# A gated-attention driver: fixed waits of TensorE's tasks replaced by the driver's own estimate

## The chip, the cores and the metric

The kernel runs on one core of a Trainium2 chip. The metric is the device time of one execution in microseconds (us), as the median of several runs. A core has five engines that matter here. TensorE (PE in the rows, its weight loads PEld) multiplies matrices out of SBUF into the banks of PSUM. VectorE (DVE) does elementwise work and scans, ScalarE (ACT) does activations and copies, GpSimd (POOL) helps with elementwise work, and SyncE (SP) issues most DMAs. Each engine runs its own list of instructions in program order and waits on semaphores for the others.

## What is computed

One inference step of a two-layer network for 128 context rows and 512 latent rows, 640 together. Each layer has a normalisation with modulation, one input projection, a neighbourhood attention, a gated linear attention (GLA) with two directions, an output projection and an MLP. The change touches only TensorE's order in the GLA. Its reference, cut to what matters:

```python
def gla_chunked(q, k, v, logf, s0):                      # chunks of 64 rows
    def step(S, inp):
        qi, ki, vi, fi = inp
        b = jnp.cumsum(fi, axis=-2)
        diff = b[..., :, None, :] - b[..., None, :, :]
        decay = jnp.exp(jnp.where(causal, diff, -jnp.inf))
        attn = jnp.einsum('bhid,bhjd,bhijd->bhij', qi, ki, decay)
        o = jnp.einsum('bhij,bhje->bhie', attn, vi) + jnp.einsum('bhid,bhde->bhie', qi * jnp.exp(b), S)
        b_last = b[..., -1:, :]
        S = jnp.exp(b_last)[..., 0, :, None] * S + jnp.einsum('bhjd,bhje->bhde', ki * jnp.exp(b_last - b), vi)
        return S, o
...
def gla_bidir(q, k, v, lf, lb, sf0, sb0):
    of, sf = gla_chunked(q, k, v, lf, sf0)
    ob, sb = gla_chunked(flip(q), flip(k), flip(v), flip(lb), sb0)
    return (of + flip(ob)).astype(v.dtype), sf, sb
```

The kernel works with chunks of 128 rows and gets the decayed products of a chunk by halving: level 64 multiplies the two halves of a chunk with each other, level 32 the halves of the halves, and so on through 16, 8, 4, 2, 1 and 0.

## The kernel before

**Projections.** A projection unit multiplies the 1024 rows of the weights of 128 output columns with the activations. It has eight steps, and each step is six matmuls, three weight loads by two parts of the 640 columns (`mm3`, L614). In the profile they write `ps_mm` from `row` and `wh` or `wl`, the high and low half of the split weights. ScalarE makes `wh` and, in the attention, VectorE makes `wl` (`prepare`, L483).

**The driver.** TensorE's order is not left to a scheduler: it is the order in which Python issues its instructions. `Drv` (L51) keeps an estimated TensorE time `dv.t`. `filler` (L119) runs a projection unit step by step, and after each step it lets waiting tasks issue their matmuls, for at most 1.8 us of estimated time. A task is a generator. Where it yields a number it comes back that many us later by `dv.t`; where it yields a name and a count it waits until so many units of that resource are free. `dv.rel(name, n, lat)` gives units back `lat` us later. The resource "sm" stands for the four small PSUM banks `ps_sm`. Which real bank a tile gets is a fixed rotation through the four.

**The estimate.** `Est` (L130) notes every instruction as it is issued and puts it into a list of slots for its engine, from a fixed cost and a cost by element; a slot may go into a hole between earlier ones. `until(tiles)` (L179) says how long from `dv.t` until the tiles are written, plus 0.6 us; `free(tiles)` (L183) says how long until their last reader is done. The tasks of the neighbourhood attention already use both; the tasks of the GLA use fixed numbers. The orders of VectorE and ScalarE come from a scheduler that sorts by priority and readiness, so they follow when TensorE's order moves.

**The GLA task.** `gla_pair` (L1129) runs for two heads at a time, twice in each layer (pair 0 and pair 1). Its steps, with the names that stand in the rows:

- gates: matmuls `ps_sm<-row,wg`, then on ScalarE and VectorE logarithms and scans into `PN`, and the scaled keys `ks`
- states, once for each direction: transposes `ps_sm<-ident,ks`, a copy to `ksT`, products `ps_sm<-gv,ksT`, and four updates of `ST` on VectorE (in layer 1 the tile lies in `cbc`, and the rows say `cbc`)
- levels 64 to 0: for each, `level_vec` (L1112) makes `ex` with two subtractions `ex<-PN`, an exponential on ScalarE and a product `ex<-ex,qk`; then TensorE multiplies `ps_sm<-ex`. Levels 64, 32 and 16 share four banks, the others take two each. `A` and `Dg` collect the results, on VectorE from level 4 on. Level 0 uses `q,qk`
- output: `ps_sm<-qs,ST` and `ps_sm<-A,gv`, then per head a sum of squares `ps_mm<-sqo,ones`

Around it run transposes of values (`ps_sm<-ident,gt` into `gv` or `V`), in layer 0 the modulation of later stages on VectorE (`ada_step`, L569, a pair of instructions `junk<-wr,cbc` and `wr<-wr,cbc`), and the rotary step of each query or key unit (`gla_rope`, L1060: a shuffle, two products and a sum on `tmp`, 512 wide).

Of the kernel before, what the change touches and what calls it, by code (L numbers as in the profile page):

```python
# [212 lines left out]
class Kern:  # L213
# [915 lines left out]
    def gla_pair(self, l, pr):  # L1129
        nc, gp, dv = self.nc, self.gp, self.dv  # L1130
# [5 lines left out]
        for d in range(2):  # L1136
            yield ("sm", 2)
            ps = [self.smp.tile([128, 512], F32, name="ps_sm", tag="sm")[:, 0:hi - lo] for lo, hi in self.HALF]
            for (lo, hi), t in zip(self.HALF, ps):
                nc.tensor.matmul(t, lhsT=self.wg[0:64, l, d, 128 * pr:128 * pr + 128],  # L1140
                                 rhs=self.zT[0:64, lo:hi], start=True, stop=True)
            dv.pe(1.07)
            bc = (PC_BGF if d == 0 else PC_BGB) + 2 * l + pr
            bcol = self.pc[:, bc:bc + 1]
            mn = gp.tile([128, T], F32, name="tmp", bufs=5)
            sp = gp.tile([128, T], F32, name="tmp", bufs=5)
            for (lo, hi), t in zip(self.HALF, ps):
                nc.scalar.activation(out=sp[:, lo:hi], in_=t, func=AF.Abs, bias=bcol)
                nc.vector.tensor_scalar(out=mn[:, lo:hi], in0=t, scalar1=bcol, scalar2=0.0, op0=ALU.add, op1=ALU.min)
            dv.rel("sm", 2, 1.4)  # L1150
            nc.scalar.activation(out=sp, in_=sp, func=AF.Exp, scale=-1.0)
            nc.scalar.activation(out=sp, in_=sp, func=AF.Ln, bias=1.0)
            if d == 0:
                for c in range(5):
                    s = slice(128 * c, 128 * c + 128)
                    nc.vector.tensor_tensor_scan(out=PN[:, 0, s], data0=mn[:, s], data1=sp[:, s], initial=0.0,
                                                 op0=ALU.add, op1=ALU.subtract)
                nc.vector.tensor_copy(tot[:, 0], PN[:, 0].rearrange("p (c t) -> p c t", c=5)[:, :, 127])
            else:
                nc.vector.memset(PN[:, 1].rearrange("p (c t) -> p c t", c=5)[:, :, 0:1], 0.0)  # L1160
                for c in range(5):
                    s = slice(128 * c, 128 * c + 127)
                    nc.vector.tensor_tensor_scan(out=PN[:, 1, 128 * c + 1:128 * c + 128], data0=sp[:, s],
                                                 data1=mn[:, s], initial=0.0, op0=ALU.add, op1=ALU.subtract)
                last = lambda t: t.rearrange("p (c t) -> p c t", c=5)[:, :, 127]
                nc.vector.tensor_tensor(out=tot[:, 1], in0=last(mn), in1=last(sp), op=ALU.subtract)
                nc.vector.tensor_tensor(out=tot[:, 1], in0=tot[:, 1], in1=last(PN[:, 1]), op=ALU.subtract)
# [5 lines left out]
        ks = gp.tile([128, 2, T], F32, name="ks", tag="ex", bufs=3)  # L1173
        cv = lambda t: t.rearrange("p (c t) -> p c t", c=5)
        nc.vector.tensor_tensor(out=cv(ks[:, 0]), in0=tot[:, 0, :, None].to_broadcast([128, 5, 128]), in1=cv(PN[:, 0]),
                                op=ALU.subtract)
# [3 lines left out]
        if l == 0:  # L1180
            ST = gp.tile([128, 2, 5, 128], F32, name="ST")
        else:

            ST = self.cbc.rearrange("p r k -> p (r k)")[:, 0:1280].rearrange("p (d c e) -> p d c e", d=2, c=5)
        nc.scalar.dma_start(out=ST[:, 0, 0], in_=self.a["state_fwd"][l, pr])
        nc.scalar.dma_start(out=ST[:, 1, 3], in_=self.a["state_bwd"][l, pr])
        vecs = {64: self.level_vec(64, PN, qk), 32: self.level_vec(32, PN, qk)}
        yield 13.0
        while not all(("gv", 2 * pr + i) in self.done for i in range(2)):
            yield 1.0  # L1190

        for d in range(2):
            chunks = (0, 1, 2, 4) if d == 0 else (3, 2, 1, 4)
            yield ("sm", 1)
            pt = self.smp.tile([128, 512], F32, name="ps_sm", tag="sm")
            for i, c in enumerate(chunks):
                nc.tensor.transpose(pt[:, 128 * i:128 * i + 128], ks[:, d, 128 * c:128 * c + 128], self.ident)
            dv.pe(0.43)
            kt = gp.tile([128, 512], F32, name="ksT", bufs=1)
            nc.scalar.activation(out=kt, in_=pt, func=AF.Copy)  # L1200
            dv.rel("sm", 1, 0.9)
            if d == 1:
                vecs[16] = self.level_vec(16, PN, qk)
            yield 1.0
            yield ("sm", 1)
            up = self.smp.tile([128, 512], F32, name="ps_sm", tag="sm")
            for i, c in enumerate(chunks):
                for hh in range(2):
                    hv = 128 * (2 * pr + hh)
                    nc.tensor.matmul(up[64 * hh:64 * hh + 64, 128 * i:128 * i + 128],  # L1210
                                     lhsT=kt[:, 128 * i + 64 * hh:128 * i + 64 * hh + 64],
                                     rhs=self.gv[:, c, hv:hv + 128], start=True, stop=True)
            dv.pe(0.95)
            for i, c in enumerate(chunks):
                u = up[:, 128 * i:128 * i + 128]
                if c == 4:
                    nc.vector.tensor_copy(ST[:, d, 4], u)
                    nc.scalar.dma_start(out=self.o["new_sf" if d == 0 else "new_sb"][l, pr], in_=ST[:, d, 4])
                else:
                    nxt = c + 1 if d == 0 else c - 1  # L1220
                    nc.vector.scalar_tensor_tensor(out=ST[:, d, nxt], in0=ST[:, d, c], scalar=dtot[:, d, c:c + 1],
                                                   in1=u, op0=ALU.mult, op1=ALU.add)
            dv.rel("sm", 1, 1.3)


        A = gp.tile([128, 10, 128], F32, name="A")
        Dg = gp.tile([128, 10, 32], F32, name="Dg")
        lv = (64, 32, 16, 8, 4, 2, 1, 0)
        qs = None
        for n, s in enumerate(lv):  # L1230

            if s == 64:
                yield ("sm", 4)
                aps = [[self.smp.tile([128, 512], F32, name="ps_sm", tag="sm") for _ in range(2)] for _ in range(2)]
            if s < 16:
                yield ("sm", 2)
                dps = [self.smp.tile([128, 512], F32, name="ps_sm", tag="sm") for _ in range(2)]
            kt, qt = vecs.pop(s)
# [36 lines left out]
                    mi = {4: 1, 2: 2, 1: 3, 0: 4}[s]  # L1275
                    nc.vector.copy_predicated(Dh, self.masks[:, mi, None, :].to_broadcast([128, 5, 32]), v5(dps[hh]))
            if s == 16:
                dv.rel("sm", 4, 1.5)
            elif s < 16:
                dv.rel("sm", 2, 0.9)  # L1280

            if n + 3 < len(lv) - 1:
                vecs[lv[n + 3]] = self.level_vec(lv[n + 3], PN, qk)
# [4 lines left out]
            elif n + 3 == len(lv):  # L1288

                qs = gp.tile([128, 2, NS], F32, name="qs", tag="ex", bufs=3)  # L1290
# [3 lines left out]
                                        in1=cv4(PN[:, 1, :NS]), op=ALU.add)  # L1294
                nc.scalar.activation(out=qs[:, 1], in_=qs[:, 1], func=AF.Exp, scale=1.0 / 16)
                nc.vector.tensor_tensor(out=qs, in0=qs, in1=qk[:, 1:2, :NS].to_broadcast([128, 2, NS]), op=ALU.mult)
            if s > 0:
                yield 2.0
        for g in range(4):
            gs = slice(32 * g, 32 * g + 32)  # L1300
            nc.vector.copy_predicated(A[gs, :, gs], self.masks[gs, 0, None, :].to_broadcast([32, 10, 32]), Dg[gs])
        self.done.add(("qk", pr))
        yield 3.0


        yield ("sm", 3)
        op = [self.smp.tile([128, 512], F32, name="ps_sm", tag="sm") for _ in range(2)]
        opp = self.smp.tile([128, 512], F32, name="ps_sm", tag="sm")
# [16 lines left out]
        for hh in range(2):  # L1325
# [1 line left out]
            nc.scalar.activation(out=og[:, :NS], in_=op[hh], func=AF.Copy)  # L1327
            nc.scalar.activation(out=og[:, NS:T], in_=opp[:, 128 * hh:128 * hh + 128], func=AF.Copy)
            ogs.append(og)
        dv.rel("sm", 3, 1.8)  # L1330
        self.done.add(("gla", pr))

        for hh in range(2):
            h = 2 * pr + hh
            og = ogs[hh]
            sq = gp.tile([128, T], F32, name="sqo", tag="tmp", bufs=5)
            nc.scalar.activation(out=sq, in_=og, func=AF.Square)
            yield 3.0
            yield ("mmx", 1)
            ps = self.mmp.tile([128, 1024], F32, name="ps_mm", tag="mm")  # L1340
            for lo, hi in ((0, 256), (256, T)):
                nc.tensor.matmul(ps[:, 256 + lo:256 + hi], lhsT=self.ones, rhs=sq[:, lo:hi], start=True, stop=True)
            dv.pe(1.07)
            rs = gp.tile([128, T], F32, name="tmp", bufs=5)
            nc.scalar.activation(out=rs, in_=ps[:, 256:896], func=AF.Ln, scale=1.0 / 128, bias=self.eps)
            dv.rel("mmx", 1, 1.2)
            nc.scalar.activation(out=rs, in_=rs, func=AF.Exp, scale=-0.5)
            nc.vector.tensor_tensor(out=og, in0=og, in1=rs, op=ALU.mult)
            while ("gate", h) not in self.done:
                yield 1.0  # L1350
            nc.vector.tensor_tensor(out=self.gg[h], in0=self.gg[h], in1=og, op=ALU.mult)
# [540 lines left out]
```

## Time and profile before

| | us |
|---|---|
| three runs | 1685.94, 1687.76, 1692.98 |
| median | 1687.76 |
| the profiled execution, as timed | 1693.68 |
| its span, first to last instruction | 1692.0 |
| TensorE busy in the span | 1621.8 |
| VectorE busy | 1228.6 |
| ScalarE busy | 749.7 |
| GpSimd busy | 424.2 |

The mean granted TensorE clock is 0.981 of full speed. TensorE's idle time is read as the length of a stretch minus its busy time. A stretch with a granted clock of 0.50 runs at 1.2 GHz instead of 2.4 GHz, so half of its busy time is lost. GLA pair 0 of layer 0 lies at about 71 to 150 us of the span, pair 1 at 151 to 235; in layer 1 they lie at 918 to 1003 and 1009 to 1083.

### The profile page before, as it was taken

The numbers are of one execution on the slowest core, as the hardware profiler recorded it, in microseconds if no ns is written. First come the engines' busy times: TensorE is split into PE (matmuls) and PEld (weight loads), VectorE is DVE, ScalarE is ACT, GpSimd is POOL, SyncE is SP. The second block draws the span as 40 slices with busy tenths as digits, with TensorE's granted clock in tenths as the row PEclk, the third lists the DMA queues.
The fourth block names the chain that finished last, engine by engine and source line by source line (L and its number), as shares of the span: only waits on it lengthen the run. The fifth ranks groups of instructions, "written<-read, shape, count | busy, mean of one in ns | idle before, by whom it ended". The sixth has DMA issues, their size and how long they took to land.

```text
span 1692.0 us, 32606 instructions
## 1 busy us (share of the span) xinstructions
PE 1621.8 (96%) x13544; PEld 1549.0 (92%) x13544; DVE 1228.6 (73%) x2300; ACT 749.7 (44%) x1224; POOL 424.2 (25%) x178
## 2 busy tenths in 40 slices
PE   8989798999999999999998899999989999999999
PEld 6988697879999999999997798988889999999998
DVE  5686968888797779777677858487796675666653
ACT  4545345644443223322345455466366444443441
POOL 1100000013344444444345000000123344343342
PEclk9998899999999999999999999999999999999999
DMA  9122243342454444444242111222221222132222
GB/s 375 52 66 79 83 144 103 98 132 97 157 178 132 154 154 148 140 149 163 78 146 67 55 54 58 95 68 76 78 71 63 74 77 88 63 100 75 76 89 87
DMA packets 61347, 179.28 MB, mean 106 GB/s; under 512 B 6928, under 2 KB 17808, under 8 KB 61200
## 3 DMA queue, kind: packets, MB, share of 16 engines
q1 hardware_dynamic: 45360, 159.76, 28.2%
q10 hardware_dynamic: 15840, 17.45, 3.4%
q8 instruction: 107, 1.75, 0.4%
q14 instruction: 40, 0.33, 0.1%
HBM read 170.36 MB, written 6.82 MB: 105 GB/s over the span
## 4 chain that ended last, share of the span: by engine, by line
PE 73%; DVE 17%; ACT 5%; issue 3%; DMA 2%; POOL 1%; ACTq 0%; DVEq 0%; POOLq 0%
PE ps_sm L198 37%; PE ps_mm L198 35%; DVE ex L198 2%; DVE s L198 2%; DVE row L198 2%; DVE sqa L198 1%; DVE wl L198 1%; ACT wh L198 1%; DVE junk L198 1%; PE ps_ss L198 1%; DVE y L198 1%; DVE wr L198 1%; ACT s L198 1%; DVE tmp L198 1%; DVE m L198 1%
## 5 line engine op out<-in xcount | busy, mean ns | idle before, releaser
L198 POOL TENSOR_TENSOR wl<-wr,wh 128x1024 fp32r<-128x1024 f32 (+1 forms) x148 | 396.3, 2683 | 1195.8 <-ACT wh L198 1184.2
L198 PE MATMUL ps_mm<-row,wh 128*128 128x256 f32 (+2 forms) x2192 | 444.8, 323 | 6.6 <-DVE row L198 3.6
L198 ACT ACTIVATE wh<-wr 128x1024 fp32r<-128x1024 f32 (+1 forms) x209 | 214.9, 1028 | 485.8 <-PE ps_sm L198 272.3
L198 PEld LDWEIGHTS ps_mm<-row,wh 128*128 128x128 f32 x2192 | 361.3, 194 | 27.4 <-issue 17.2
L198 PE MATMUL ps_mm<-row,wl 128*128 128x256 f32 (+2 forms) x1096 | 258.2, 314 | 0.5 <-DVE wl L198 0.5
L198 PEld LDWEIGHTS ps_mm<-row,wl 128*128 128x128 f32 x1096 | 202.8, 193 | 0.7 <-DVE wl L198 0.7
L198 PE MATMUL ps_sm<-row,wh 128*128 128x322 f32 (+2 forms) x736 | 153.9, 312 | 0.0
L198 ACT ACTIVATE r<-r 128x512 f32<-128x512 f32 (+2 forms) x192 | 113.7, 618 | 59.8 <-DVE r L198 57.0
L198 DVE SCALAR_TENSOR_TENSOR ar<-ar,cbc 128x1024 f32<-128x1024 f32 x56 | 124.9, 2238 | 1.0
L198 PEld LDWEIGHTS ps_sm<-row,wh 128*128 128x128 f32 x736 | 122.3, 190 | 0.0
L198 PE MATMUL ps_sm<-uh,wh 128*128 128x256 f32 (+1 forms) x512 | 119.0, 308 | 0.0
L198 PE MATMUL ps_mm<-uh,wh 128*128 128x256 f32 (+1 forms) x512 | 118.9, 308 | 0.0
L198 PE MATMUL ps_mm<-ul,wh 128*128 128x256 f32 (+1 forms) x512 | 118.6, 308 | 0.0
L198 PE MATMUL ps_sm<-ul,wh 128*128 128x256 f32 (+1 forms) x512 | 118.5, 307 | 0.0
L198 PE MATMUL ps_mm<-uh,wl 128*128 128x256 f32 (+1 forms) x512 | 118.5, 307 | 0.0
L198 PE MATMUL ps_sm<-uh,wl 128*128 128x256 f32 (+1 forms) x512 | 118.5, 307 | 0.0
L198 DVE SCALAR_TENSOR_TENSOR row<-ps_sm,mod,row 128x256 f32<-128x256 f32 (+1 forms) x216 | 81.6, 430 | 50.2 <-PE ps_sm L198 50.2
L198 DVE TENSOR_TENSOR r<-ps_sm,r 128x322 f32<-128x322 f32 x98 | 46.9, 490 | 93.6 <-PE ps_sm L198 55.4
L198 DVE SCALAR_TENSOR_TENSOR row<-ps_mm,mod,row 128x128 f32<-128x128 f32 (+2 forms) x180 | 89.1, 533 | 31.0 <-PE ps_mm L198 31.0
L198 PE MATMUL ps_sm<-m,wh 128*128 128x322 f32 x480 | 99.2, 312 | 0.0
L198 PE MATMUL ps_sm<-row,wl 128*128 128x322 f32 (+2 forms) x368 | 99.0, 311 | 0.0
L198 DVE TENSOR_TENSOR wl<-wr,wh 128x1024 fp32r<-128x1024 f32 (+2 forms) x69 | 73.2, 1061 | 30.5 <-ACT wh L198 29.6
(222 smaller groups left out, 3067.4 us busy)
## 6 DMA issues: line engine op xcount, KB each, us to landing
wr<-w_dn SPq DMA_DIRECT2D x68, 512.0 KB, 3.5
wr<-w_up SPq DMA_DIRECT2D x64, 512.0 KB, 3.5
ar<-w_ada SPq DMA_DIRECT2D x56, 512.0 KB, 3.7
wr<-w_in SPq DMA_DIRECT2D x48, 512.0 KB, 3.6
wr<-w_ada SPq DMA_DIRECT2D x24, 512.0 KB, 3.5
wa<-w_ada SPq DMA_DIRECT2D x16, 512.0 KB, 10.2
wr<-w_o SPq DMA_DIRECT2D x16, 512.0 KB, 3.5
tab<-bias ACTq DMA_DIRECT2D x32, 96.0 KB, 2.9
```

Source lines behind the costliest of these rows:

```text
L198: r = f(*args, **kw)
```

## The change

All waits of `gla_pair` that were numbers become calls of the estimate. The two waits that stood at the end of a level (2.0 us, and none ahead of level 64) become one ahead of each level, for that level's own `ex` tiles. `dv.pe` and all arithmetic stay as they are.

```diff
-            dv.rel("sm", 2, 1.4)
+            dv.rel("sm", 2, self.est.free(*ps))
...
-        yield 13.0
+        yield self.est.until(ks)
...
-            dv.rel("sm", 1, 0.9)
+            dv.rel("sm", 1, self.est.free(pt))
             if d == 1:
                 vecs[16] = self.level_vec(16, PN, qk)
-            yield 1.0
+            yield self.est.until(kt)
...
-            dv.rel("sm", 1, 1.3)
+            dv.rel("sm", 1, self.est.free(up))
...
         for n, s in enumerate(lv):
+            yield self.est.until(*vecs[s])
...
             if s == 16:
-                dv.rel("sm", 4, 1.5)
+                dv.rel("sm", 4, self.est.free(*aps[0], *aps[1]))
             elif s < 16:
-                dv.rel("sm", 2, 0.9)
+                dv.rel("sm", 2, self.est.free(*dps))
...
-            if s > 0:
-                yield 2.0
...
-        yield 3.0
+        yield self.est.until(A, qs, ST)
...
-        dv.rel("sm", 3, 1.8)
+        dv.rel("sm", 3, self.est.free(*op, opp))
...
-            yield 3.0
+            yield self.est.until(sq)
...
-            dv.rel("mmx", 1, 1.2)
+            dv.rel("mmx", 1, self.est.free(ps))
```

**First place: TensorE, layer 0, pair 0, where the scaled keys are transposed.** Before, the transposes of the value tile `gt` stand alone, and those of `ks` come seven projection steps later:

```order
L198 MATMUL ps_mm<-row_7_278,wh 128x384
L198 MATMUL ps_mm<-row_6_277,wl 128x256
L198 MATMUL ps_mm<-row_6_277,wl 128x384
L198 MATMUL ps_sm<-ident,gt 128x128 x5
L198 MATMUL ps_mm<-row_0_279,wh 128x256
```

Now the same place reads:

```order
 L198 MATMUL ps_mm<-row_6_277,wl 128x256
 L198 MATMUL ps_mm<-row_6_277,wl 128x384
+L198 MATMUL ps_sm<-ident,gt 128x128 x4
+L198 MATMUL ps_sm<-ident,ks 128x128 x4
+L198 MATMUL ps_sm<-ident,gt 128x128
+L198 MATMUL ps_mm<-row_0_279,wh 128x256
```

The transposes of `ks` moved seven steps of six matmuls forward, in between those of `gt`.

**Second place: VectorE, layer 0, pair 0, between the state updates and level 8.** Before, the last two updates of `ST` stand behind steps of the rotary work of the next key unit (`tmp`):

```order
L198 SCALAR_TENSOR_TENSOR ST<-ST,dtot,ps_sm 128x128 x2
L198 STREAM_SHUFFLE tmp<-tmp 128x512
L198 SCALAR_TENSOR_TENSOR ST<-ST,dtot,ps_sm 128x128
L198 TENSOR_TENSOR tmp<-tmp,sin 128x512
L198 TENSOR_TENSOR tmp<-tmp,cos 128x512
L198 TENSOR_TENSOR ex<-ex,qk 128x1280
L198 TENSOR_TENSOR qk<-tmp 128x512
L198 COPY ST<-ps_sm 128x128
```

Now all of `ST` stands ahead of this, and the rotary work falls between the vectors of levels 8 and 4 (the first `ex<-ex,qk` is level 8's product, the second level 4's):

```order
L198 SCALAR_TENSOR_TENSOR wr,mod_110<-wr,cbc 128x1024
L198 TENSOR_TENSOR ex<-PN 128x640 x2
L198 TENSOR_TENSOR wl<-wr,wh 128x1024
L198 TENSOR_TENSOR ex<-PN 128x640
L198 TENSOR_TENSOR ex<-ex,qk 128x1280
L198 TENSOR_TENSOR ex<-PN 128x640
L198 STREAM_SHUFFLE tmp<-tmp 128x512
L198 COPY A<-ps_sm 128x512
L198 TENSOR_TENSOR tmp<-tmp,sin 128x512
L198 TENSOR_TENSOR tmp<-tmp,cos 128x512
L198 TENSOR_TENSOR ex<-ex,qk 128x1280
```

The state moved out from behind the rotary work, and level 4's product moved behind it.

**Third place: TensorE, layer 1, pair 0, level 8 at the same projection step.** Before, level 8 stands here alone, with transposes of `gt` on both sides, and level 4 comes three steps later:

```order
L198 MATMUL ps_mm<-row_2_9007,wl 128x384
L198 MATMUL ps_sm<-ident,gt 128x128 x4
L198 MATMUL ps_sm<-ex 32x32 x40
L198 MATMUL ps_sm<-ident,gt 128x128 x5
L198 MATMUL ps_mm<-row_4_9009,wh 128x256
```

Now (40 of the 80 are level 8, 40 are level 4):

```order
L198 MATMUL ps_mm<-row_2_9007,wl 128x256
L198 MATMUL ps_mm<-row_2_9007,wl 128x384
L198 MATMUL ps_sm<-ex 32x32 x80
L198 MATMUL ps_mm<-row_4_9009,wh 128x256
L198 MATMUL ps_mm<-row_4_9009,wh 128x384
```

Level 4 moved up behind level 8, with no projection step between them, and the transposes of `gt` moved away.

## Rows read from the trace of the kernel before

**Rows 1.** The page's first line: the span of the profiled execution.
```profile
span 1692.0 us, 32606 instructions
```

**Rows 2.** Windows, by stage: length, then busy (count) of PE, PEld, DVE, ACT, POOL; PEclk.
```profile
82.60:138.90 56.30, 48.12 (x877) 44.53 (x875) 50.66 (x81) 24.16 (x33) 0.00 (x0) 0.94 0.26 82
152.20:220.70 68.50, 57.99 (x923) 52.84 (x922) 62.02 (x104) 33.55 (x50) 0.00 (x0) 0.90 0.26 84
941.40:986.00 44.60, 41.93 (x836) 38.49 (x834) 34.37 (x58) 16.70 (x24) 0.00 (x0) 0.96 0.17 53
1009.00:1070.00 61.00, 57.71 (x945) 53.46 (x946) 49.77 (x82) 32.34 (x50) 0.00 (x0) 0.97 0.19 59
250.00:400.00 150.00, 138.14 (x1062) 120.99 (x1060) 128.13 (x348) 77.67 (x167) 11.73 (x5) 0.97 0.35 110
1105.00:1205.00 100.00, 96.16 (x795) 82.63 (x794) 81.19 (x248) 62.96 (x143) 2.37 (x1) 1.00 0.27 83
```

**Rows 3.** TensorE's waits, 82 to 225 us: us in total, times, longest us.
```profile
PE ps_sm L198 <- DVE ST L198: 12.6, 3, 5.8
PE ps_sm L198 <- DVE V L198: 2.5, 1, 2.5
PE ps_sm L198 <- DVE A L198: 1.7, 1, 1.7
PE ps_sm L198 <- DVE Dg L198: 1.3, 2, 1.1
```

**Rows 4.** TensorE's waits, 941.4 to 1075 us.
```profile
PE ps_sm L198 <- DVE cbc L198: 2.5, 2, 1.3
PE ps_sm L198 <- DVE A L198: 2.0, 1, 2.0
```

**Rows 5.** Windows of the stretches in which TensorE's clock was lowered.
```profile
101.90:108.60 6.70, 5.61 (x36) 5.19 (x44) 4.00 (x6) 1.27 (x1) 0.00 (x0) 0.50 0.03 10
139.50:149.60 10.10, 10.10 (x51) 8.98 (x51) 0.82 (x1) 2.15 (x5) 0.00 (x0) 0.50 0.11 36
180.40:190.60 10.20, 4.49 (x21) 4.40 (x22) 8.05 (x13) 3.34 (x5) 0.00 (x0) 0.50 0.36 118
207.70:211.00 3.30, 3.30 (x89) 2.90 (x89) 3.23 (x7) 1.58 (x2) 0.00 (x0) 0.50 0.02 5
1047.40:1050.70 3.30, 3.30 (x83) 2.89 (x83) 3.26 (x6) 1.27 (x1) 0.00 (x0) 0.50 0.34 134
```

**Rows 6.** Timeline of TensorE: level 64's second part, a gate stage, one level.
```profile
102.99 0.48 PE L198 MATMUL ps_sm<-ex 64*64 64x64 f32 x6 [4.56 <-DVE ST L198]
...
1008.88 2.42 PE L198 MATMUL ps_sm<-row,wg 64*128 64x256 f32 x8
...
1027.16 0.60 PE L198 MATMUL ps_sm<-ident,ks 128*128 128x128 f32 x4
...
1041.02 0.89 PE L198 MATMUL ps_sm<-ex 64*32 64x32 f32 x80
```

**Rows 7.** Window of 18 projection steps (108 matmuls), of tile ps_mm alone.
```profile
1011.20:1027.40 16.20, 16.10 (x108) 15.84 (x108) 0.00 (x0) 2.73 (x4) 1.00 0.09 35
```

**Rows 8.** Groups of VectorE's instructions, 82 to 140 us: busy, mean ns.
```profile
L198 DVE TENSOR_TENSOR ex<-PN 128x640 f32<-128x640 f32 x13 | 10.5, 849 | 2.2 <-PE ps_sm L198 2.2
...
L198 DVE SCALAR_TENSOR_TENSOR junk<-wr,cbc 128x1024 bf16<-128x1024 f32 x4 | 4.9, 1216 | 0.0
...
L198 DVE SCALAR_TENSOR_TENSOR ST<-ST,dtot,ps_sm 128x128 f32<-128x128 f32 x6 | 2.0, 340 | 0.0
```

**Rows 9.** Timeline of VectorE in layer 1, pair 1.
```profile
1022.41 1.48 DVE L198 TENSOR_TENSOR ks<-ks,qk 128x1280 f32<-128x1280 f32 x1
1023.81 1.48 DVE L198 TENSOR_TENSOR ex<-ex,qk 128x1280 f32<-128x1280 f32 x1
1025.21 1.21 DVE L198 TENSOR_TENSOR wl<-wr,wh 128x1024 fp32r<-128x1024 f32 x1
1026.35 1.48 DVE L198 TENSOR_TENSOR ex<-ex,qk 128x1280 f32<-128x1280 f32 x1
```

## The prediction

> **What bounds the kernel now.** I began with the page and went to the stages that the change touches. The profiled execution has a span of 1692.0 us [rows 1] and was timed at 1693.68; the median of the three runs shown is 1687.76, some 6 us less. I make the sum in us gained or lost against this one execution and take it off the median as it stands.
>
> The windows by stage [rows 2] show what can be won. TensorE's idle time is the length less its busy time. In GLA pair 0 of layer 0 (82.6 to 138.9) that is 56.30 - 48.12 = 8.18 us, in pair 1 68.50 - 57.99 = 10.51, in layer 1 2.67 and 3.29: 24.65 us together. The same rows show who is late: VectorE is busy 50.66 of 56.30 us and 62.02 of 68.50 in layer 0. In layer 1, which has no modulation work there, it is 34.37 of 44.60 and 49.77 of 61.00. So in layer 0 TensorE waits beside a VectorE that is nearly full; TensorE's order can move such waits, but it can only remove those in which VectorE did something that nobody was waiting for.
>
> The lists of TensorE's waits say the same by name. In layer 0, 12.6 us are for `ST` [rows 3], in three pieces of which one is 4.56 at 102.99 [rows 6]. That is level 64 waiting for the bank whose last reader is the state update. `V` (2.5), `A` (1.7) and `Dg` (1.3) follow [rows 3]. In layer 1 the waits are `cbc`, the state again, with 2.5, and `A` with 2.0 [rows 4].
>
> The third thing to read is the clock. Five stretches by these waits ran at a granted 0.50, the lower level of 1.2 GHz [rows 5]. Half of their busy time is lost: 5.61 / 2 = 2.8 and 10.10 / 2 = 5.05 by pair 0, 2.25 and 1.65 by pair 1, 1.65 in layer 1. The 10.10 is the whole output stage of pair 0, which follows the wait for `A` of 1.7. The losses now are thus 8.18 + 2.8 + 5.05 = 16.0, 10.51 + 3.9 = 14.4, 2.67, and 3.29 + 1.65 = 4.94: 38.0 us. Nothing before 82 us moves, and behind the GLA the order is the same again, so all of the change's effect lies in these 38 us and in what takes their place.
>
> **The prices.** A projection step costs 16.10 / 18 = 0.9 us [rows 7], a level of 32-row products 0.9, a set of key transposes 0.6, a gate stage 2.4 [rows 6]; I take a state product as a level, 0.9. On VectorE a subtraction for a level costs 10.5 / 13 = 0.8, a modulation instruction 1.2, a state update 0.3, and so does a `Dg` copy by its nearness [rows 8]. A level's product costs 1.4 from start to start (1022.41 to 1023.81), a `wl` 1.14 [rows 9]. A 512-wide step is an estimate from the 640-wide one, four fifths of 0.8, or 0.65. With these I walk down the changed order of TensorE and VectorE side by side. Where VectorE's sum is longer than TensorE's between the same two points, the difference is a wait.
>
> **Layer 0, pair 0.** The keys are transposed seven steps earlier, level 64 stands three steps earlier (53 instead of 56, in steps from the start of the projections) and the output seven (73 instead of 80). All state updates now stand ahead of the rotary work, so the 4.56 us and the low clock behind it go; about 0.4 remain, inside the rounding. New waits come at the levels. From level 64 to level 4 VectorE has two modulation instructions, four subtractions, one `wl`, two products and four 512-wide steps, now that the rotary work stands ahead of level 4's product: 2.4 + 3.2 + 1.14 + 2.8 + 2.6 = 12.1 us. TensorE has four levels, level 64 taken as one of them, and five steps: 3.6 + 4.5 = 8.1. It waits 4.0, shared by levels 8 and 4. To level 2: 0.65 + 3.2 + 1.4 = 5.25 against 0.9 + 2.7 = 3.6, a wait of 1.65. To level 0, which now stands right behind level 1 and needs the banks that level 2's `Dg` copies free: 1.4 + 0.9 + 0.5 + 2.4 + 1.14 + 2.3 = 8.6 against 0.9 + 4.5 + 0.9 = 6.3, a wait of 2.3. To the output both have 8.0. That is 8.0 us of waits. Each is as long as those that were followed by a lowered clock, but while TensorE is waiting for VectorE anyway a slow TensorE only shortens the next wait; I count one low stretch, the last, with 1.65. The output's 5.05 I take as gone, since hardly any wait is left ahead of `A`; its other bound is that all of it stays. Pair 0 loses 9.7 instead of 16.0: **a gain of 6.3**.
>
> **Layer 0, pair 1.** Here the keys come 11 steps behind the gates instead of 14. From the gate matmuls (1008.88) [rows 6] to the end of the keys' product (1022.41 + 1.48) [rows 9] layer 1 needed 15.0 us with much the same VectorE list. TensorE has 2.4 + 11 x 0.9 = 12.3: a wait of 2.7, where there was none, and 1.65 of clock. Up to the last state update VectorE has five subtractions, two `wl`, three products, two modulation pairs, a gate product and eight small ones: 4.0 + 2.3 + 4.2 + 4.8 + 0.8 + 2.4 = 18.5, against 12.0 of TensorE (nine steps, transposes, state products, the first part of level 64) and 1.65 for the low clock. So level 64 still waits, 4.8, and 1.65 of clock follow. Level 2 then gets the two banks of a value transpose. VectorE copies the second of them to `V` only after eight subtractions and four products, 19.5 in all, against 15.3: 4.2 and 1.65. Together 16.65 instead of 14.4: **a loss of 2.25**.
>
> **Layer 1.** In pair 0 levels 8 and 4 now follow each other with no step between. VectorE needs 3.2 + 2.8 + 0.65 + 1.14 = 7.8 for both, and some 0.8 for ScalarE's exponential, against 6.3: a wait of 2.3, 1.65 of clock, 0.4 at level 2, or 4.35 instead of 2.67. In pair 1 the keys come 11 steps behind the gates instead of 18; the 15.0 us were measured here, and VectorE's list between is unchanged, so the wait is 2.7, with 1.65 of clock. The second value transposes wait 2.45 for the banks of the first. That is 6.8 instead of 4.94. **Losses of 1.7 and 1.9.**
>
> The rest of the diff has one answer: the wait ahead of the sums of squares and the bank returns move matmuls that stand in projection work with nobody behind them, and SyncE's and GpSimd's lists are unchanged.
>
> **Sum.** 6.3 - 2.25 - 1.7 - 1.9 = 0.45 us gained: 1692.0 becomes 1691.6 of span, and 1687.76 becomes 1687.3. The measurement tells apart about 0.5%, or 8.4 us, so this is no change.
>
> **The rivals.**
>
> *The estimate holds (faster).* The neighbourhood attention already takes its waits from this estimate. In layer 1 it idles 3.84 of 100 us, in layer 0 11.86 of 150 beside a VectorE that is busy 128.13 [rows 2]. If the GLA's 230.4 us came to the first share, idle time would fall from 24.65 to 8.8, and clock losses of 13.4 in proportion by 8.6: 24.4 us, or 1663.4. At the second share it is 6.4 + 3.5 = 9.9, or 1677.9. Against it: the neighbourhood tasks have several independent units to choose from, a GLA pair is one chain. Chance 0.20.
>
> *Each new wait costs the clock as well (slower).* I count twelve new waits, and six low stretches as hidden. If these are not hidden, 6 x 1.65 = 9.9 us come on top, and if the output of pair 0 stays at 1.2 GHz, 5.05: 15 us, or 1702. The output and three of the six are enough to make it measurably slower (8.4 + 0.45 = 8.9). For it speaks that waits of 1.7 and 2.0 have such a stretch behind them [rows 3 to 5]; against it, that the slowed work lies ahead of a further wait for VectorE. The Trainium skill (Perfetto Trace Analysis, Matmul Optimizations) says that the engine scales with its use and that matmuls should stand back to back in batches; the rows agree, and by it alone this rival would be the likelier. Chance 0.18.
>
> *The banks decide (nothing happens).* Of the 18.7 us in layer 0's waits, 12.6 + 2.5 + 1.3 = 16.4 end with the reader of a small bank, not with a missing operand [rows 3]. Four banks in fixed rotation may keep every wait at its size wherever it stands: 1687.8. The Trainium skill (Perfetto Trace Analysis, Optimization Strategy) reads gaps that repeat as a sign that PSUM or SBUF is short for the next tile; by this rule the order brings nothing. Against it: the 4.56 us came from VectorE's order. Chance 0.17.
>
> **How the numbers follow.** The forecast has 0.45. With the banks' rival it makes 0.62 for no measurable change, 0.20 for faster, 0.18 for slower. The range takes the lower half of the gain at the second share, some 4 us below 1677.9 for my rounding, down to 1674, and the slower rival's beginning, up to 1697.
>
> **What would show it.** Right: level 64 of layer 0's pair 0 waits under 1 us for `ST`; the output stage there runs at full clock; both second pairs show a wait of 2 to 3 us at `ps_sm<-ident,ks`; layer 1 has a wait of about 2 us at level 4 of pair 0. Wrong: no wait at the keys (then the estimate holds), idle time in the four stretches far from 24.65, or the output stage of layer 0's pair 0 still at a granted 0.50.

## The result

The changed kernel takes 1702.47 us (median of four runs, 1701.51 to 1703.7), the kernel before 1688.83 in the same rounds. The ratio is 1.0075 with a 95% interval of 1.0055 to 1.0094; six later runs gave 1.0056 (1.0037 to 1.0075). The change makes the kernel 9 to 13 us slower, and both intervals lie above 1. The forecast was no change, 1687.3, and the time lies above its range of 1674 to 1697.

The page of the changed kernel, against [rows 1]:

```profile
span 1701.8 us, 32594 instructions
```

Its windows, first at the four places of [rows 2] (moved where the gates start later), then each layer from its first gate matmul to the start of the key and query transposes behind the GLA. Columns as in [rows 2]:

```profile
82.60:138.90 56.30, 51.12 (x906) 47.51 (x905) 49.63 (x80) 23.07 (x33) 0.00 (x0) 0.91 0.26 81
149.90:220.70 70.80, 58.32 (x940) 52.97 (x939) 60.16 (x100) 31.52 (x47) 0.00 (x0) 0.90 0.25 81
941.60:986.00 44.40, 39.73 (x833) 37.02 (x831) 33.44 (x57) 16.14 (x22) 0.00 (x0) 0.96 0.17 53
1014.30:1076.00 61.70, 56.15 (x934) 51.42 (x933) 48.96 (x79) 31.65 (x48) 0.00 (x0) 0.94 0.18 58
71.53:256.97 185.44, 162.49 (x2174) 149.97 (x2173) 148.61 (x247) 87.81 (x131) 0.00 (x0) 0.93 0.28 88
917.63:1111.43 193.80, 176.90 (x2297) 164.78 (x2296) 131.06 (x210) 93.12 (x140) 5.17 (x2) 0.96 0.19 63
```

The same two layer windows of the kernel before:

```profile
71.42:256.67 185.25, 165.06 (x2174) 151.35 (x2173) 148.34 (x247) 87.12 (x131) 0.00 (x0) 0.92 0.27 88
917.41:1101.68 184.27, 175.01 (x2297) 162.68 (x2296) 130.83 (x210) 92.82 (x140) 5.17 (x2) 0.98 0.21 66
```

Layer 0 is as long as before (185.44 and 185.25). Layer 1 is 9.5 us longer: TensorE's idle time grew from 184.27 - 175.01 = 9.26 to 193.80 - 176.90 = 16.90, and its busy time by 1.9.

What TensorE waits for, layer 0 (71.5 to 257 us) and then layer 1 (945 to 1111), against [rows 3] and [rows 4]; columns: us in total, times, longest:

```profile
PE ps_sm L198 <- DVE ST L198: 6.4, 1, 6.4
PE ps_mm L198 <- ACT sqo L198: 4.4, 2, 2.2
PE ps_sm L198 <- DVE ex L198: 3.7, 2, 2.4
PE ps_sm L198 <- DVE V L198: 3.0, 2, 1.7
PE ps_sm L198 <- DVE ks L198: 2.3, 1, 2.3
...
PE ps_mm L198 <- ACT sqo L198: 3.4, 2, 2.8
PE ps_sm L198 <- DVE ks L198: 2.8, 1, 2.8
PE ps_sm L198 <- DVE V L198: 2.8, 2, 1.5
PE ps_sm L198 <- DVE Dg L198: 2.1, 1, 2.1
PE ps_sm L198 <- DVE ex L198: 1.5, 1, 1.5
```

Keys (`ks`), values (`V`) and levels (`ex`, `Dg`) are there as forecast. `sqo`, the square ahead of the sums of squares, is not among the forecasts and not in [rows 3] or [rows 4]: 4.4 + 3.4 = 7.8 us in four waits, all ahead of the second sum of a pair.

ScalarE and then TensorE around the first of the four (start, length, what, idle time before it and its releaser):

```profile
135.65 0.28 ACT L198 ACTIVATE row<-ps_sm 128x128 f32<-128x128 f32 x1
135.80 0.75 ACT L198 ACTIVATE sqo<-row 128x640 f32<-128x640 f32 x1
139.59 0.80 ACT L198 ACTIVATE tmp<-ps_mm,eps 128x640 f32<-128x640 f32 x1 [3.04 <-PE ps_mm L198]
140.28 1.05 ACT L198 ACTIVATE wh<-wr 128x1024 fp32r<-128x1024 f32 x1
141.23 0.73 ACT L198 ACTIVATE tmp<-tmp 128x640 f32<-128x640 f32 x1
141.85 0.72 ACT L198 ACTIVATE sqo<-row 128x640 f32<-128x640 f32 x1
...
138.31 1.24 PE L198 MATMUL ps_mm<-sqo,ones 128*128 128x256 f32 x4
...
142.63 2.24 PE L198 MATMUL ps_mm<-sqo,ones 128*128 128x256 f32 x4 [2.21 <-ACT sqo L198]
```

This is the theory for the experiments (**theory S**). The source writes the second head's square behind the first head's logarithm and exponential, and ScalarE's list has it there. The logarithm waits for TensorE's first sum; then come a weight copy, the exponential and the square, which starts at 141.85 although the last part of its input (`row`) was written at 135.9 and ScalarE idled 3.04 us in between. By its code the driver's estimate may put a new instruction into a hole between earlier ones, so for it the square is done early, and it lets the second sum go one projection step behind the first instead of three. TensorE's whole list then waits. In the kernel before, the square stood behind the first head's logarithm as well, but the second sum came three steps later and found it written (two sums on TensorE, and the square on ScalarE):

```profile
152.26 1.34 PE L198 MATMUL ps_mm<-sqo,ones 128*128 128x256 f32 x4
...
157.57 1.24 PE L198 MATMUL ps_mm<-sqo,ones 128*128 128x256 f32 x4
...
155.59 0.73 ACT L198 ACTIVATE sqo<-row 128x640 f32<-128x640 f32 x1
```

In layer 1 the same happens with other work ahead of the square (`wh`, then `gg` and `tmp`), here ScalarE and then TensorE:

```profile
998.79 1.06 ACT L198 ACTIVATE wh<-wr 128x1024 fp32r<-128x1024 f32 x1 [1.67 <-PE ps_mm L198]
999.76 0.78 ACT L198 ACTIVATE gg<-ps_mm,pc 128x640 f32<-128x640 f32 x1
1000.43 0.69 ACT L198 ACTIVATE tmp<-ps_mm 128x640 f32<-128x640 f32 x1
1001.01 0.73 ACT L198 ACTIVATE sqo<-row 128x640 f32<-128x640 f32 x1
...
1001.80 1.34 PE L198 MATMUL ps_mm<-sqo,ones 128*128 128x256 f32 x4 [2.75 <-ACT sqo L198]
```

### The profile page after: what moved, and what is told of

It reads as the page before. It is cut to its first block, busy times and chain, and to the rows that moved or that the text cites. A ratio compares the mean times of both kernels' runs of the same rounds, so it can differ in the third digit from the quotient of the medians.

```text
span 1701.8 us, 32594 instructions
## 1 busy us (share of the span) xinstructions
PE 1621.4 (95%) x13544; PEld 1550.1 (91%) x13544; DVE 1231.5 (72%) x2300; ACT 751.0 (44%) x1224; POOL 424.5 (25%) x178
## 4 chain that ended last, share of the span: by engine, by line
PE 72%; DVE 18%; ACT 5%; issue 3%; DMA 2%; POOL 1%; DVEq 0%; ACTq 0%; POOLq 0%
PE ps_sm L198 36%; PE ps_mm L198 34%; DVE ex L198 3%; DVE row L198 2%; DVE s L198 2%; DVE sqa L198 1%; ACT wh L198 1%; DVE wl L198 1%; PE ps_ss L198 1%; DVE y L198 1%; ACT s L198 1%; DVE wr L198 1%; DVE junk L198 1%; DVE tmp L198 1%; ACT tmp L198 1%
```

## The experiments

All ratios are to the kernel before in the same rounds (medians 1688.8 to 1691.4), with 95% intervals. "Layer" columns are the windows from gates to transposes, in one profiled execution each: length and, behind it, TensorE's idle time. Where a run leaves a layer as it was before, its row shows how far such a length repeats: layer 0 took 185.25, 182.20 and 183.23 (before, e10, e14), layer 1 between 182.99 and 185.74 (before, e7, e8, e11, e12). So a single length is good to some 3 us.

| | us | ratio | layer 0 | layer 1 |
|---|---|---|---|---|
| before | | 1 | 185.25, 20.19 | 184.27, 9.26 |
| the change | 1702.47 | 1.0075 (1.0055 to 1.0094) | 185.44, 22.95 | 193.80, 16.90 |
| e1 sums fixed | 1690.0 | 0.9996 (0.9985 to 1.0007) | 179.50, 18.84 | 186.84, 14.33 |
| e2 keys fixed | 1700.41 | 1.0054 (1.0042 to 1.0066) | 187.27, 23.96 | 189.82, 13.42 |
| e3 levels fixed | 1682.15 | 0.995 (0.9936 to 0.9964) | 171.36, 14.78 | 192.16, 14.23 |
| e4 banks fixed | 1694.23 | 1.0011 (0.9998 to 1.0024) | 178.41, 18.87 | 191.69, 13.90 |
| e5 squares early | 1691.89 | 1.0016 (1.0005 to 1.0028) | 178.73, 17.84 | 190.41, 15.83 |
| e6 before + sums | 1696.01 | 1.0038 (1.0023 to 1.0052) | 185.68, 20.70 | 188.59, 13.14 |
| e7 layer 0 only | 1688.22 | 0.9995 (0.9985 to 1.0005) | 181.55, 22.37 | 184.21, 9.18 |
| e8 e7 + levels fixed | 1679.05 | 0.994 (0.9921 to 0.9958) | 172.41, 14.39 | 184.09, 9.05 |
| e9 before + keys | 1687.26 | 0.9984 (0.997 to 0.9998) | 177.17, 17.65 | 185.30, 10.30 |
| e10 layer 1 only, sums fixed | 1694.89 | 1.0022 (1.001 to 1.0034) | 182.20, 20.30 | 186.80, 13.32 |
| e11 e8 + sums fixed | 1680.96 | 0.9941 (0.9926 to 0.9956) | 174.42, 16.14 | 185.74, 9.13 |
| e12 e8 + squares early | 1680.76 | 0.9941 (0.9921 to 0.996) | 172.36, 14.24 | 182.99, 10.57 |
| e13 the change again | 1701.14 | 1.0056 (1.0037 to 1.0075) | 182.03, 24.20 | 193.61, 16.55 |
| e14 layer 1 only | 1700.48 | 1.0056 (1.0035 to 1.0076) | 183.23, 20.24 | 193.77, 16.56 |

### One part of the change set back

**e1**, the sums of squares:

```diff
-            yield self.est.until(sq)
+            yield 3.0
```

> The changed kernel with one wait set back: the one ahead of each head's sum of squares is the fixed 3.0 us again. On TensorE only the second sum of each pair moves (from one to four projection steps behind the first, in layer 1's pair 0 from four to eight). Theory S (the second square stands on ScalarE behind the first sum's logarithm, a weight copy and an exponential, and the estimate does not see this): the waits of 2.21, 2.21, 2.75 and 0.62 us for sqo go, and the lowered clock behind 142.9 and 1003.1 us with them. Their sum is 7.8 us of idle time and 3.3 of clock; if layer 0's part is swallowed later as it was in the changed kernel, 3.4 + 1.65 = 5.0 remain. So 1691.4 to 1697.5 us against 1702.5. Rival L (the loss sits in the levels, the keys and the value transposes): the sum of squares only delays the same wait, and it stays above 1700.

Measured 1690.0, no difference from before: the whole loss is gone with this one wait, a little more than theory S asked for. The list of waits has no `sqo` any more; the entries for the other tiles stay within 0.7 us, and one of 0.9 for `tmp` comes in layer 0. The longest of them, layer 0 first and then layer 1:

```profile
PE ps_sm L198 <- DVE ST L198: 6.0, 1, 6.0
PE ps_sm L198 <- DVE ex L198: 3.7, 2, 2.5
PE ps_sm L198 <- DVE V L198: 3.0, 2, 1.7
PE ps_sm L198 <- DVE ks L198: 1.8, 1, 1.8
...
PE ps_sm L198 <- DVE ks L198: 2.8, 1, 2.8
```

Idle time fell by 4.1 in layer 0 and 2.6 in layer 1. Rival L falls as the cause of the loss.

**e2**, the keys:

```diff
-        yield self.est.until(ks)
+        yield 13.0
```

> The changed kernel with one wait set back: the keys are transposed 13.0 us after their task is issued, as before. Theory K (the keys are asked for 7 to 11 projection steps too early): the waits of 2.26 us (164.4) and 2.78 us (1029.4) for ks go, the wait of 6.37 for ST in layer 0 shrinks to about the 5.8 of before, and the lowered clock behind 1030.4 goes: 2.8 + 1.65 = 4.4 us in layer 1 and up to 2.8 in layer 0, so 1695 to 1698 against 1702.5. Rival S (the sums of squares make the loss): no more than 2 us less, 1700 or above, since the second sum still stands one step behind the first. Rival L (the levels): the later keys push the level waits together, 1702 or more.

Measured 1700.41. The wait for `ks` went, but a wait of 3.62 us for `ex` at 1054.5 and 2.85 for `A` at 137.6 took its place. Theory K falls, rival S holds.

**e3**, the levels:

```diff
-            yield self.est.until(*vecs[s])
...
+            if s > 0:
+                yield 2.0
```

> The changed kernel with the waits of the levels set back: none ahead of a level, 2.0 us behind each. Theory L (a level is asked for as soon as the estimate has its operands, ahead of VectorE's real list): the waits of 1.04, 1.53 and 2.10 us in layer 1 go, 4.7 us, and 2.4 + 1.3 + 1.5 in layer 0 with one low stretch at 122.5; layer 1 alone gives 1697.8, both 1691. Rival S: the second sums of squares come later or sooner by chance and decide; levels alone give at most 2 us, 1700.5 or above.

Measured 1682.15, 20 us less than the change and 8.5 less than before. This is more than theory L had, and by the traces 14.1 us of it lie in layer 0 (171.36 instead of 185.44) and 1.6 in layer 1. So the levels aren't what makes layer 1 long, but estimated levels throw away a gain in layer 0. Not all of it is theirs: with the levels one of layer 0's two waits for `sqo` went, and the other fell to 1.5 us.

**e4**, the banks: the seven `dv.rel` delays back to numbers, such as

```diff
-        dv.rel("sm", 3, self.est.free(*op, opp))
+        dv.rel("sm", 3, 1.8)
```

> The changed kernel with the seven fixed delays of the returns of the banks set back (1.4, 0.9, 1.3, 1.5, 0.9, 1.8, 1.2 us) and all waits for operands still estimated. Theory B (banks are given back too early by the estimate, and transposes of values are put into banks that are still read): the 1.50 + 1.27 us for V at 1059.7 and the 1.30 + 1.73 at 200.3 go with their low clock, so about 4.4 us less in layer 1 alone, 1698, and 1693 with both. Theory S and K (operands, not banks): levels move by one or two steps and nothing else, 1700.5 to 1704.5.

Measured 1694.23, as theory B had it, but not for its reason alone. One of the seven delays, 1.2 us, is that of the bank of the sums themselves; with it the second sum comes a step or more later, and the waits for `sqo` are 1.34 and 1.87 us instead of four with 7.8. The waits for `V` went as well, and one of 2.06 for `mod` came. What each is worth isn't separated here.

### Is it the square, or TensorE's order?

**e5** leaves TensorE's order exactly as the change has it and moves only ScalarE's squares:

```diff
+        sqs = []
+        for og in ogs:
+            sq = gp.tile([128, T], F32, name="sqo", tag="tmp", bufs=5)
+            nc.scalar.activation(out=sq, in_=og, func=AF.Square)
+            sqs.append(sq)
...
-            sq = gp.tile([128, T], F32, name="sqo", tag="tmp", bufs=5)
-            nc.scalar.activation(out=sq, in_=og, func=AF.Square)
+            sq = sqs[hh]
```

> The changed kernel with all its waits, but both squares of a pair are issued to ScalarE ahead of the loop over the heads, so the second no longer stands behind the first sum's logarithm. TensorE's order is instruction by instruction that of the changed kernel; only ScalarE's changes. Theory S: the second sum, still one step behind the first, finds its square ready; the waits of 2.21, 2.21 and 2.75 us and two low stretches go as with the fixed wait: 1688 to 1694 against 1702.5. Rival O (what helped in the run before was TensorE's order, three more steps between the sums, not the square): the bank or the logarithm is what the second sum waits for, the waits stay above 1.5 us each and the time above 1699.

Measured 1691.89. ScalarE and then TensorE at the place shown above for the change:

```profile
135.35 0.75 ACT L198 ACTIVATE sqo<-row 128x640 f32<-128x640 f32 x1
...
135.98 0.75 ACT L198 ACTIVATE sqo<-row 128x640 f32<-128x640 f32 x1
139.12 0.80 ACT L198 ACTIVATE tmp<-ps_mm,eps 128x640 f32<-128x640 f32 x1 [2.40 <-PE ps_mm L198]
...
137.85 1.24 PE L198 MATMUL ps_mm<-sqo,ones 128*128 128x256 f32 x4
...
139.97 1.34 PE L198 MATMUL ps_mm<-sqo,ones 128*128 128x256 f32 x4
```

Both squares are done by 136.8, in ScalarE's idle time, and the second sum starts without a wait, still one step behind the first. TensorE's order was not at fault by itself; rival O falls. The mechanism of theory S is shown. The repair isn't complete: 1.0016 lies some 3 us above before. In layer 1 both waits for `sqo` went too, but one of 1.05 for `tmp` came behind the second sum, at 990.98, and idle time fell only from 16.90 to 15.83.

**e6** is the kernel before with the sums' wait alone changed.

```diff
-            yield 3.0
+            yield self.est.until(sq)
```

> The kernel before with one edit of the change alone: the estimate ahead of each sum of squares, all other waits fixed. In layer 0 the second sum moves from three steps behind the first to one, in layer 1's pair 0 from six to two, in its pair 1 it stays two behind. Theory S: layer 0 gets two waits of about 2.2 us, layer 1 one of about 2.7, with 0 to 3 low stretches of 1.65: 7 to 12 us slower than before, 1697 to 1702. Rival L (the second sum only waits because levels and outputs were moved up as well): under 3 us, below 1693.

Measured 1696.01, 6.4 us slower by the ratio, just under theory S's 7 to 12. Layer 1 has the wait at full size, and is 4.3 us longer:

```profile
999.89 1.62 PE L198 MATMUL ps_mm<-sqo,ones 128*128 128x256 f32 x4 [2.76 <-ACT sqo L198]
```

In layer 0 the wait was 0.61 in pair 0, where a gate stage stands between the two sums, and none above 0.4 in pair 1. In pair 1 the transposes of values and one step stand between the sums. So the two waits of 2.2 us that theory S expected in layer 0 did not come by this edit alone; that they need the new place of the outputs too is argued, not tested.

### Which layer

In e7, e8, e10, e11, e12 and e14 `gla_pair` stands twice in the code, and each layer calls its own.

**e7**, all of the change in layer 0 and none in layer 1.

> The estimate in layer 0's two pairs only; layer 1 has the fixed waits of before. Theory by layers: at the start of the key and query transposes behind the pairs, before and after stood level in layer 0 (256.7 and 257.0 us), and all of the loss came between 917 and 1124 us, so 1702.5 - 9.8 = 1692.7, or 1689 to 1694 beside a kernel before at 1689 to 1691. Rival C (the loss is in the clock, which falls in other places of each execution, and not in layer 1's order): 1697 or more.

Measured 1688.22, level with before and a little below the 1689 to 1694 of the theory by layers; rival C asked for 1697 or more. **e14** is the reverse, and **e13** the change itself again:

> The estimate in layer 1 only; layer 0 has the fixed waits of before. Theory by layers: all of the loss is here. By the traces' stretch from gates to transposes it is 193.80 - 184.27 = 9.5 us, 1699 to 1701; by the medians it is the whole change without layer 0's 0.9995, 1.008, 1703. Of it 3.5 are levels, keys and banks, as the run with the sums' fixed wait in layer 1 showed, the other 6 the sums of squares. Rival A (the layers do not add, since the change in layer 0 shifts what layer 1 meets): below 1696.

> The changed kernel itself, to have it in the same rounds as the estimate in layer 1 alone. It was 1.0075 of before in four runs. Theory by layers: again 1.006 to 1.009, 1700 to 1705 beside a kernel before at 1690. Rival C (part of it was the clock's, whose low stretches fall at other places in other executions): 1.003 to 1.005, 1695 to 1699.

1.0056 each: layer 1 alone costs as much as the whole change, and 0.9995 + 1.0056 - 1 = 1.0051 lies within e13's interval. The layers add; rival A falls. In the three executions that have the change in layer 1 this layer took 193.80, 193.61 and 193.77 us, so its 9.5 us repeat, and e14's time is the one that they gave (1699 to 1701). By its time e13 is where the theory by layers had it, by its ratio between that and rival C: the change's own size is good to some 3 us.

**e10**, the change in layer 1 without the sums:

> The estimate in layer 1 only, and there with the fixed 3.0 us ahead of the sums of squares; layer 0 has the fixed waits of before. It leaves what the change does in layer 1 besides the sums: keys 11 steps behind the gates, levels 8 and 4 together, banks. Theory R (my prediction's terms for layer 1 hold without the sums): 3.6 us slower than before, 1692 to 1695 beside 1689 to 1691; by the run with the sums' wait set back in both layers it was 186.84 - 184.27 = 2.6. Rival S+ (the sums were all of layer 1's loss): no difference, below 1691.5.

1.0022, or 3.7 us (1.7 to 5.7 by the interval; 2.5 by the two traces, 186.80 and 184.27). Its waits in layer 1 are the forecast ones:

```profile
PE ps_sm L198 <- DVE ks L198: 2.8, 1, 2.8
PE ps_sm L198 <- DVE V L198: 2.8, 2, 1.5
PE ps_sm L198 <- DVE Dg L198: 2.1, 1, 2.1
PE ps_sm L198 <- DVE ex L198: 1.6, 1, 1.6
```

So of layer 1's 0.0056, 0.0022 are keys, values and levels and 0.0034, 5.7 us, the sums (good to some 4 us; 7.0 by the traces, 193.77 and 186.80). For layer 0, e1 less e10 gives 0.9996 - 0.0022 = 0.9974, a gain of 4.4 us without the sums (good to some 3 us, from two intervals), which the sums take back to 0.9995 (e7).

### A version that beats both

**e8**: the estimate in layer 0 only, and there with fixed levels (the edit of e3).

> The estimate in layer 0 only, and there with the levels' fixed 2.0 us; layer 1 has the fixed waits of before. In the run with fixed levels layer 0 was 13.5 us shorter than before (the transposes behind it start at 243.2 instead of 256.7 us) and layer 1 7.9 us longer (192.2 instead of 184.3 from gates to transposes). If the two layers add, the second goes and the first stays: 1682 - 7.9 = 1674, and 1673 to 1678 is expected. Rival P (layer 0's gain came from where the sums and value transposes of that run happened to fall, with layer 1's order needed for neither): the same 1674. Rival C (part of the gain is only the clock's): above 1680.

1679.05, 0.6% faster than before; the expected 1673 to 1678 was missed by 1 us, though the profiled execution took 1675.19. Its two layers:

```profile
70.74:243.15 172.41, 158.02 (x2173) 144.75 (x2173) 147.91 (x247) 86.54 (x131) 0.00 (x0) 0.98 0.30 95
899.05:1083.14 184.09, 175.04 (x2297) 162.59 (x2297) 130.83 (x210) 92.87 (x140) 5.18 (x2) 0.98 0.21 66
```

Against the profiled execution of before, which was a long one (1693.68), layer 0 is 12.8 us shorter; by the ratio it is 10.1. Of the 12.8, 5.8 are idle time and 7.0 TensorE's busy time, at a mean granted clock of 0.98 instead of 0.92.

**e9**, the keys' wait alone:

```diff
-        yield 13.0
+        yield self.est.until(ks)
```

> The kernel before with one edit of the change alone: the transposes of the keys wait by the estimate instead of 13.0 us; levels, banks and sums of squares keep their fixed waits. In layer 0 the keys move from 51 and 97 projection steps to 44 and 93, in layer 1's pair 1 from 18 steps behind the gates to 11. Theory K+ (what the change gains is the keys' earlier place in layer 0, and with fixed levels it is not given back): the 4.56 us for ST and the low clock at 101.9 go, 4.6 + 2.8, and as in the two runs with fixed levels some 6 more in pair 1; layer 1's pair 1 pays 2.8 + 1.65 for ks: 9 us faster than before, 1679 to 1684. Rival (my prediction's sizes): 4.6 + 2.8 gained, 2.7 + 1.65 lost in each of two pairs, no change, 1688 to 1692.

1687.26, slightly faster (0.9984, or 2.7 us), between theory K+ and its rival. In layer 0's pair 0 the 4.56 for `ST` went, but in pair 1 it waits 4.33 and 2.45 for `ST`, and both second pairs pay for `ks` (2.25 and 2.78).

**e11** (e8 with the edit of e1) and **e12** (e8 with the edit of e5):

> As the best run so far (estimate in layer 0 only, its levels on the fixed 2.0 us), and in addition the fixed 3.0 us ahead of the sums of squares. In pair 0 nothing moves but the second sum; in pair 1 the keys come two steps sooner (94 instead of 96) and level 64 seven (101 instead of 108), because other banks are free. Theory W (the gain of pair 1 came from level 64's late place, behind VectorE's state updates, and not from the keys): the wait for ST, 1.25 us there, is back at 5 to 6, and with one or two low stretches it is 1684 to 1688. Rival S (the sums of squares still cost 1.5 us there): 1676 to 1679.

> As the best run so far, with both squares of a pair issued to ScalarE ahead of the loop over the heads; TensorE's order stays but for a few rows. Theory S: the wait of 1.51 us for sqo (221.7) goes and nothing else moves: 1677 to 1679. Rival: the squares push ScalarE's copies of value tiles back by 0.7 us, and TensorE waits for those instead: 1680 to 1682.

By the ratio neither differs from e8. In us both lie some 2 above what theory S expected of them, beside a kernel before that was 1.7 slower too. In e11 the wait for `ST` came back as theory W said,

```profile
171.08 0.32 PE L198 MATMUL ps_sm<-ex 64*64 64x64 f32 x2 [1.80 <-DVE ST L198]
...
175.84 0.48 PE L198 MATMUL ps_sm<-ex 64*64 64x64 f32 x6 [4.43 <-DVE ST L198]
```

but layer 0 was only 2.0 us longer, while waits of 1.57 for `ksT`, 1.51 for `sqo` and 0.99 inside a level went at the same time. The 1684 to 1688 of theory W did not come, so as an account of the gain it falls. In e12 the wait for `sqo` went, and one of 2.63 for `ks` and one of 1.94 for `V` came, so by its waits the rival was nearer. What exactly makes e8 faster than before, the waits or the clock that follows them, isn't settled. How much of it is the levels alone can be told where no sum waits: layer 0 without the sums is 0.9974 with estimated levels (e1 less e10) and 0.9941 with fixed ones (e11), so fixed levels are worth 0.0033, 5.6 us (good to some 4). The rest of what lies between e7 and e8 (9.3 us) is argued to go with the sums' waits, which moved; the intervals don't settle it.

## Why the prediction was wrong

**The step that failed** is "the rest of the diff has one answer: the wait ahead of the sums of squares and the bank returns move matmuls that stand in projection work with nobody behind them", costed at nothing. Everything on TensorE is behind a waiting matmul there, since its list runs in order; I had looked for an engine that waits for the sum, and not for what the sum waits for. I walked VectorE's list beside TensorE's at every other edit, and ScalarE's at none. The cost was 7.8 us of waits, and two low-clock stretches right behind them (behind the first 2.21 and the 2.75). These two windows, and the sum over the eight stretches of the two layers that ran at the lower clock (a ninth, at 941.7, stands in the kernel before at the same place and is left out in both):

```profile
142.90:146.30 3.40, 3.40 (x11) 2.68 (x11) 1.25 (x2) 1.36 (x2) 0.00 (x0) 0.51 0.47 154
1003.10:1006.50 3.40, 3.40 (x15) 3.40 (x14) 2.40 (x3) 1.58 (x3) 0.00 (x0) 0.50 0.25 101
...
sum 37.40, PE 31.57 PEld 29.78 DVE 27.86 ACT 12.39 POOL 0.00; mean PE 3.95 PEld 3.72 DVE 3.48 ACT 1.55 POOL 0.00
```

Half of 3.40 twice is 3.4 more, 11.2 in all, against a loss of 9 to 13. In e13's execution of the same kernel the four waits are again 7.8 us and two low stretches stand behind them. In e1 and e5, where only this is taken out, the ratio is 0.9996 and 1.0016: the "no change" that was forecast for the rest.

**The rest, term by term.** The four signs that the prediction named for being right all came: no wait for `ST` at level 64 of layer 0's pair 0, its output stage at full clock, 2.26 and 2.78 us at the keys, 1.53 at level 4 of layer 1's pair 0. None of them looked at the sums of squares, whose four waits lie behind the four stretches. Idle time in the four stretches was forecast as 8.0, 2.7 + 4.8 + 4.2 = 11.7, 2.3 + 0.4 = 2.7 and 2.7 + 2.45 = 5.15, together 27.5. Measured, length less busy time of the first four windows above: 5.2, 12.5, 4.7 and 5.5, together 27.9. That the sums agree so well is luck: the first stretch was forecast 2.8 too high, the third 2.0 too low.

- Layer 0, pair 0: the `ST` wait of 4.56 went, as said, and the output stage runs at full clock. The waits at the levels were 1.30 + 2.38 at levels 8 and 4 (forecast 4.0), none at level 2 (1.65) and 1.50 at level 0 (2.3). In e13, where no low stretch stood there, level 2 waited 1.57 us and began at the same time (112.75 against 112.78): the slow TensorE took the place of a wait, as the prediction argued.
- Layer 0, pair 1: keys 2.26 (forecast 2.7), level 64 6.37 (4.8), `V` 3.0 (4.2).
- Layer 1, pair 0: 1.53 at level 4 (forecast 2.3), 2.10 at level 2 (0.4), and 1.04 inside level 16, for which the profile shows no cause: together clearly more than the 2.7. The 0.8 us for ScalarE's exponential in this sum stood on no row; the twelve of layer 1 in the kernel before (941 to 1075 us) took 1.27 on average.
- Layer 1, pair 1: keys 2.78 (2.7), `V` 2.77 (2.45).
- The layers: a gain of 6.3 - 2.25 = 4.05 was forecast for layer 0 and 4.4 measured without the sums; a loss of 3.6 for layer 1, and 3.7 measured in e10. This is closer than the measurement can tell, and partly luck: in e10's trace layer 1 has 4.1 us more idle time than before, where the forecast had 1.9, and 1.5 us less busy time, where it had 1.65 more for the clock.
- The clock: 9.9 us were forecast. The eight low stretches had a busy time of 31.57 (the sum line above), half of it 15.8; 3.4 of these lie behind the sums. In e13 there were only six, with 10.5, of which again 3.4 behind the sums: this term changes by 5 us from one execution to the next.

The output stage's window, with its granted clock of 1.00 (0.50 in [rows 5]):

```profile
128.00:138.00 10.00, 10.00 (x84) 8.96 (x83) 4.81 (x9) 5.01 (x9) 0.00 (x0) 1.00 0.54 172
```

**The rivals.** "Each new wait costs the clock as well" gave up to 1702, and the time is 1702.5, but not for that reason: in this execution the clock's losses rose from 13.4 to 15.8, 2.4 of about 13 us, and in e13, which took as long (1701.18), they were 10.5, less than before. And the output of pair 0 ran at full clock. The Trainium skill (Perfetto Trace Analysis, Matmul Optimizations) wants matmuls back to back because the engine scales its power with its use; the two low stretches above agree with that, but by these sums the waits themselves weigh more than the clock behind them. "The banks decide" fails: `ST` in pair 0 and `V` moved. "The estimate holds" fails in the change and comes nearest in layer 0 with fixed levels. A rival that asks whether the estimate's picture of an engine's list is the real one was missing, though it stood in the text of the estimate that a slot may go into a hole.

## What to carry to other kernels

Where a planner's estimate replaces a margin, ask of each awaited instruction what stands ahead of it in its engine's real list, and whether the estimate lets it overtake. A wait of an in-order engine is never "with nobody behind it": its own list is behind it. When such an optimistic wait is found, there are two repairs. Issuing the operand earlier in the source (e5) brought the ratio to 1.0016, a longer wait (e1) to 0.9996.

## What was not expected of the hardware

With the same order on TensorE, layer 0 took 185.44 us in the profiled execution of the change and 181.55 and 182.03 in e7 and e13:

```profile
71.15:252.70 181.55, 159.18 (x2173) 146.92 (x2172) 148.40 (x247) 87.74 (x131) 0.00 (x0) 0.95 0.28 90
...
71.90:253.93 182.03, 157.83 (x2173) 145.89 (x2172) 148.53 (x247) 87.94 (x131) 0.00 (x0) 0.96 0.27 90
```

The idle time is nearly the same (22.95, 22.37, 24.20); the busy time is not (162.49, 159.18, 157.83), and the mean granted clock is 0.93, 0.95 and 0.96. The same waits have a stretch at the lower level (1.2 GHz) behind them in one execution and not in another: the wait of 2.38 us at level 4 of layer 0's pair 0 stood in a stretch at 0.50 from 105.4 to 112.2, the one of 2.48 at the same place in e13 in a stretch at 1.00. The Trainium skill (TensorE: Matmul & The Clock Gate, Part 1) calls the clock's warm-up at the start of a kernel run-variable for one and the same kernel; these rows show such a variation in the middle of one, with up to 3.9 us in a layer. So a loss of clock read from one execution is good to a few us only, while idle time repeats within 2. A profiled execution may lie 4 to 6 us from its kernel's median (e8: 1675.19 and 1679.05; the kernel before: 1693.68 and 1687.76).
